# Odd tokens' rows through VectorE's block transposes, short matmuls inside products, and the first up operands queued one product earlier

## The chip, the core and the metric

The kernel runs on one core of one Trainium2 chip. A core has a matmul engine (TensorE, PE in the profile, with its weight loads as PEld), VectorE (DVE), ScalarE (ACT), GpSimd (POOL) and SyncE (SP); SP and POOL here mostly issue DMAs, and sixteen DMA engines carry these out. The metric is device time in microseconds (us) of one execution. The kernel before takes 1544.23 us, the median of three runs (1544.19 to 1544.71).

## What is computed

One decoder layer over 1024 tokens of 1024 channels, in float32. Cut to what matters here:

```python
m = jax.nn.sigmoid(sa) * y_a + jax.nn.sigmoid(sb) * y_b
x = x + jnp.einsum("bsd,de->bse", m, w_o[l])

h = rms_norm(x, g_mlp[l])
f = jnp.square(jax.nn.relu(jnp.einsum("bsd,df->bsf", h, w_1[l])))
x = x + jnp.einsum("bsf,fd->bsd", f, w_2[l])
return rms_norm(x, g_final)
```

`rms_norm` divides each token's row by the root of its mean square and multiplies by a gain per channel. Ahead of this stand a normalisation, one wide projection, a convolution branch and a recurrent branch, which give `y_a`, `y_b`, `sa` and `sb`; the change doesn't touch them. The stretch in question is the end of the `w_o` product, the second `rms_norm`, and the start of the up product with `w_1`.

## The kernel before, in words

**Layout.** In this stretch channels lie on the 128 partitions and tokens along the free axis, even tokens apart from odd ones. The residual x after the `w_o` product is held as `x1[kk, o, c2]`: kk is the half of the channels, o is 0 for even and 1 for odd tokens, c2 a pair of channel blocks; each tile is 128 x 1024 and holds two channel blocks of 512 tokens.

**Products.** A matrix product is computed as a two-by-two block product with seven products in place of eight (right blocks: channel half kk by token parity o). For each group i of output channels the products have the numbers p = 1, 2, 6, 7, 4, 5, 3. The left operands of p = 5, 6, 7, 3 are sums of weight blocks (`g_sums`, `up_lhs`), the right operands of p = 6, 7, 4, 5 differences of x blocks (`g_t`: numbers 1 to 4 of these differences).

**Precision.** Every float32 operand is split into a high part (rounded to the matmul's format) and the low rest. One product of one group is twelve matmuls over four channel blocks: high by high, high by low, low by high. For left operands ScalarE writes the negated high part, GpSimd issues a DMA that adds the source onto it (this gives the low part), and ScalarE writes the high part (`split_dma`, L63 to L67; in the profile ACT L65, POOL L66, ACT L67). For right operands ScalarE writes the high part and VectorE subtracts (`g_parts`, L1216 and L1063), except the up stage's second (gu2l, gu2h), which goes by `split_dma`.

**The sequence.** `gseq` lists 64 steps: 28 for `w_a_out` ("a"), 28 for `w_o` ("o"), and 8 for the up product ("u": p = 1 and 2 for the first four groups). The order of everything on ScalarE, VectorE, TensorE and the DMA queues is that of the program text. At step n the loop issues what follows product n - 1 (`g_post`), then product n's matmuls (`g_mm`), then the left operands of product n + 4 (`g_lhs`), the left sums of n + 5, then the extra work that the table `GX` lists for that step. Some VectorE work goes first into a list (`later`) that is sorted by an expected ready time and issued by `vector_work` or `flush`. In the names of the profile go3e is the bank of group 3 in the "o" stage, gu1a that of group 1 in the "u" stage; go_5 or gu_2 are left operands, gu1h and gu1l the right operand's two parts. After the 64 steps the up stage goes on with f0b, f1b, f0c and so on (`up_step`, L1550), product 6 first.

**The even tokens' rows and statistics.** While the "o" products run, ScalarE squares finished blocks of even x (`x1_sq`) and VectorE adds the squares (`x1_add`). At step 20 and 21 VectorE turns 32 x 32 blocks of even x (`x1_turn`, L462 STREAM_TRANSPOSE) into tiles x1r, and SP writes them with sixteen DMAs (L1394), four per tile, to `x1d` in DRAM, in runs of 128 floats; the down stage reads these rows much later. Four matmuls against a column of ones add the squares over channels (`x1_cols`, cs). `x1_root` and `x1_diag` form 1/rms by token on diagonal blocks (rdm, on VectorE and ScalarE), `x1_spread` multiplies ones with these blocks, so that each partition has every token's factor (rbm), and `x1_normed` scales x in place on VectorE (L462).

**The odd tokens' rows and statistics.** `x1_rows` does this in another way, at the first "u" step: 32 TensorE transposes into eight PSUM banks (tr), ScalarE squares each bank with a sum along the row (L1418), VectorE copies each bank into a row tile (L1422), SP writes four tiles of 128 x 1024 (L1426). Root, diagonal, spread and scaling follow as for the even ones.

**Buffers.** Most 128 x 1024 tiles come from one pool of 37 buffers:

```python
tp = ctx.enter_context(tc.tile_pool(name="acts", bufs=37))
def T(name, dt=F32, shape=(P, S)):
    return tp.tile(list(shape), dt, tag="T", name=name)
```

A new tile takes a buffer whose last tile is no longer used in the program text; the first instruction that writes it waits until the last reader of the old tile has ended, a DMA included. Which buffer a tile gets follows from the order of the requests. Eight DMA semaphores each for SP and POOL go around: a DMA is issued when the one eight before it has landed.

Of the kernel before, what the change touches and what calls it, by code (L numbers as in the profile page):

```python
# [24 lines left out]
EPS = 1e-6  # L25
# [5 lines left out]
def trunk_kernel(ctx: ExitStack, tc: tile.TileContext, x, xt_in, xt_eo, vecs, w_in, w_a_out, w_b_out,  # L31
                 w_rg, w_o, w_1, w_2, g_final, out):

    nc = tc.nc
    cp = ctx.enter_context(tc.tile_pool(name="consts", bufs=1))
# [8 lines left out]
    def T(name, dt=F32, shape=(P, S)):  # L44
        return tp.tile(list(shape), dt, tag="T", name=name)
# [8 lines left out]
    HALVES = (slice(0, HS), slice(HS, S))  # L54
# [52 lines left out]
    ident = cp.tile([P, P], F32, name="ident")  # L107
# [4 lines left out]
    ones = cp.tile([P, P], F32, name="ones")  # L112
# [671 lines left out]
    for i in range(2, NZ):  # L784
        n = zseq.index((i, 1))
# [18 lines left out]
    with tc.manual_schedule(engines=ENGINES):  # L804
        for s in range(3, NC1):
# [25 lines left out]
            c = CH[s - 1]  # L831
# [19 lines left out]
            for d in range(5):  # L851
                if s - d in EXP:
                    g = EXP[s - d]
# [36 lines left out]
    def EV(name):  # L890
        return vp.tile([P, HS], F32, tag="ev", name=name)
# [167 lines left out]
    def bank(name):  # L1059
        return zp.tile([P, HS], F32, tag="z", name=name)  # L1060
# [158 lines left out]
    def g_t(w, c2, *ns):  # L1219

        r = g_right[w]
        if 2 in ns:
            r[6, c2] = T(f"gt2{w}{c2}")
        b11, b12, b21, b22 = (r[kk, o, c2] for kk in range(2) for o in range(2))
# [41 lines left out]
    def g_mm(w, i, p):  # L1266
        b = {1: "a", 2: "a", 6: "b", 5: "e", 3: "e", 7: "f", 4: "f"}[p]
        if p in (1, 5):
            gb[w, i, b] = bank(f"g{w}{i}{b}")
        o, n = go.pop((w, i, p)), 0  # L1270
        for k in range(4):
            h, l = (a[w, p, k // 2][:, HALVES[k % 2]] for a in (gh, gl))
            for a, b_ in ((o[:, 0, k, :], h), (o[:, 0, k, :], l), (o[:, 1, k, :], h)):
                nc.tensor.matmul(gb[w, i, b], a, b_, start=p in (1, 5) and n == 0, stop=n == 11,  # L1274
                                 skip_group_check=p not in (1, 5))
                n += 1
        at("P", 12 * MM)
# [92 lines left out]
    x1d = dp.tile([8, P, D], F32, name="x1d")  # L1370


    sqs = []

    def x1_sq(i, m_):
        s = EV(f"sq{i}{m_}")
        nc.scalar.activation(s, x1[i // 2, 0, i % 2][:, HALVES[m_]], AF.Square)
        sqs.append((at("A", 0.62, clk["V"]), s))

    def x1_add(n=1):  # L1380
        for _ in range(n):
            ready, s = sqs.pop(1)
            later(ready, 0.63, tt, sqs[0][1], sqs[0][1], s, ALU.add)

    def x1_turn(kk):
        for th in range(2):
            r = T(f"x1r{kk}{th}")
            for c2 in range(2):
                src = x1[kk, 0, c2].rearrange("p (m h b j) -> p h m b j", m=2, h=2, j=32)[:, th]
                dst = r.rearrange("p (b m j) -> p m b j", m=4, j=32)[:, 2 * c2:2 * c2 + 2]  # L1390
                dve(0.65, 0, nc.vector.transpose, dst, src)
            d = x1d[2 * th:2 * th + 2].rearrange("q (b i) (k g x) -> k g i (q b) x", b=4, k=2, g=4)
            for g in range(4):
                nc.sync.dma_start(d[kk, g], r[32 * g:32 * g + 32].rearrange("p (b x) -> p b x", x=P))  # L1394

    def x1_cols():

        sqs.append(bank("cs"))
        for n in range(4):
            nc.tensor.matmul(sqs[1][:, n:n + 1], sqs[0][1][:, n * P:(n + 1) * P], ones[:, 0:1],  # L1400
                             start=True, stop=True)
        at("P", 0.9)

    def x1_rows(*ts):
        for t in ts:
            o, n = divmod(t, 4)
            if n == 0:
                rst[o] = cp.tile([P, 6, 4], F32, tag="st6", name=f"stm{o}", bufs=2)
            rows = T(f"x1r{t}")
            for kk in range(2):  # L1410
                ps = bank(f"tr{t}{kk}")
                for c in range(4):
                    nc.tensor.transpose(ps[:, c * P:(c + 1) * P],
                                        x1[kk, o, c // 2][:, c % 2 * HS + n * P:c % 2 * HS + (n + 1) * P],
                                        ident)
                at("P", 0.45)
                a = T(f"sq{t}{kk}")[:, 0:HS]
                nc.scalar.activation(a, ps, AF.Square, accum_out=rst[o][:, kk, n:n + 1])  # L1418
                at("A", 0.63, clk["P"])

                def copy(rows, kk, ps, t):
                    nc.vector.tensor_copy(  # L1422
                        rows[:, HALVES[kk]].rearrange("p (g c j) -> p c g j", g=4, c=4),
                        ps.rearrange("p (c g j) -> p c g j", g=4, c=4))
                    if kk:
                        nc.sync.dma_start(x1d[t], rows)  # L1426

                later(clk["P"], 0.63, copy, rows, kk, ps, t)
            if t == 7:
                x1_root(1)  # L1430
            if o:
                vector_work(clk["V"])

    def x1_root(o):

        if o == 0:
            rst[o] = cp.tile([P, 6, 4], F32, tag="st6", name=f"stm{o}", bufs=2)
        a, b, v, s = (rst[o][:, i, :] for i in range(4))
        if o:
            tt(v, a, b, ALU.add)  # L1440
        nc.vector.tensor_scalar(v, v if o else sqs[1][:, 0:4], 1.0 / D, EPS, ALU.mult, ALU.add)
        nc.scalar.activation(s, v, AF.Sqrt)
        at("A", 1.5)

# [163 lines left out]
    def flush():  # L1608
        vector_work(clk["V"])

    def g_get(n, f):
        return f(*gseq[n]) if 0 <= n < len(gseq) else None

# [17 lines left out]
        13: ((g_parts, "o", 4, 1),), 14: ((x1_sq, 0, 0),),  # L1631
        15: ((g_parts, "o", 5, 0), (x1_sq, 1, 0)),
        16: ((g_parts, "o", 5, 1), (x1_add,), (x1_sq, 2, 0), (up_load, 0, (0,))),
        17: ((g_parts, "o", 3, 0), (x1_add,), (x1_sq, 3, 0), (x1_sq, 0, 1), (up_load, 1, (0,))),
        18: ((g_parts, "o", 3, 1), (x1_add, 2), (x1_sq, 1, 1), (up_load, 2, (0,))),
        19: ((x1_add,), (x1_sq, 2, 1), (up_load, 3, (0,))),
        20: ((x1_add,), (x1_sq, 3, 1), (flush,), (x1_turn, 0)),
        21: ((x1_add,), (flush,), (x1_cols,), (x1_turn, 1), (up_load, 0, (1,))),
# [174 lines left out]
    ready = 4  # L1813
# [285 lines left out]
```

## Time and profile before

| what | value |
|---|---|
| median of three runs | 1544.23 us |
| the profiled execution's own time | 1544.64 us |
| its span, first to last instruction | 1542.9 us |
| granted TensorE clock | 0.999 |
| busy: TensorE, VectorE, ScalarE, GpSimd | 1533.1, 1222.5, 903.6, 184.4 us |
| first "u" product starts | 914.91 us |
| first product of the up stage proper (f0b) starts | 943.11 us |

Start times are microseconds from the span's start. A row of the view in order of time gives the start, the duration, the engine, the line, the operation, output <- input, the shape, how many were merged, and in brackets how long the engine stood idle before it and what ended that. A row of the DMA view gives the queue's engine, the count, KB of each and the median time from issue to landing; rows that begin with q0 or q1 give the two DMA queues' packets, MB and share of the sixteen engines' time in the stretch asked for. Matmuls overlap, so the time that one costs is the distance between starts: 0.23 us for 512 columns, not its duration of 0.39.

### The profile page before, as it was taken

The numbers are of one execution on the slowest core, as the hardware profiler recorded it, in microseconds if no ns is written. First come the engines' busy times: TensorE is split into PE (matmuls) and PEld (weight loads), VectorE is DVE, ScalarE is ACT, GpSimd is POOL, SyncE is SP. The second block draws the span as 40 slices with busy tenths as digits, with TensorE's granted clock in tenths as the row PEclk, the third lists the DMA queues.
The fourth block names the chain that finished last, engine by engine and source line by source line (L and its number), as shares of the span: only waits on it lengthen the run. The fifth ranks groups of instructions, "written<-read, shape, count | busy, mean of one in ns | idle before, by whom it ended". The sixth has DMA issues, their size and how long they took to land.

```text
span 1542.9 us, 19178 instructions
## 1 busy us (share of the span) xinstructions
PE 1533.1 (99%) x6782; PEld 1262.4 (82%) x6782; DVE 1222.5 (79%) x1648; ACT 903.6 (59%) x1261; POOL 184.4 (12%) x219
## 2 busy tenths in 40 slices
PE   9999999999999999999999999999999999999998
PEld 8888788888888888888888887888888888888886
DVE  6899999979899997478569879755555558888897
ACT  6648576567567667345275777554444475555553
POOL 0000000002222222000022332000000001111110
PEclk9999999999999999999999999999999999999999
DMA  8776978898997879953579898333333779888862
GB/s 347 197 189 161 251 187 222 217 280 217 247 253 196 193 191 246 327 157 116 182 201 299 197 193 204 137 122 112 113 114 111 241 216 228 223 222 224 209 130 110
DMA packets 132288, 307.82 MB, mean 200 GB/s; under 512 B 13232, under 2 KB 35248, under 8 KB 132192
## 3 DMA queue, kind: packets, MB, share of 16 engines
q1 hardware_dynamic: 101744, 230.60, 46.0%
q0 software_dynamic: 30304, 75.74, 26.9%
q8 instruction: 53, 0.87, 0.2%
q14 instruction: 43, 0.35, 0.1%
q10 hardware_dynamic: 144, 0.26, 0.0%
HBM read 147.69 MB, written 58.72 MB: 134 GB/s over the span
## 4 chain that ended last, share of the span: by engine, by line
PE 95%; DMA 2%; issue 1%; DVE 1%; SPq 0%; POOL 0%; ACT 0%; POOLq 0%; DVEq 0%
PE z L726 18%; PE d L1863 15%; PE yb L1097 8%; PE e L1983 3%; PE keep L1863 2%; PE z L258 1%; PE rg L534 1%; PE rg L536 1%; PE rg L535 1%; DMA x<-in_x_dram 1%; DMA gu<-w_raw 1%; DMA xc<-in_xt_dram 0%; PE go3f L1274 0%; PE f15d L1550 0%; PE f15c L1550 0%
## 5 line engine op out<-in xcount | busy, mean ns | idle before, releaser
L726 PE MATMUL z<-xh,win_h 128*128 128x512 f32 x400 | 124.9, 390 | 0.0
L726 PE MATMUL z<-xl,win_h 128*128 128x512 f32 x400 | 124.5, 389 | 0.0
L1875 DVE TENSOR_TENSOR acc<-acc,d 128x1024 f32<-128x1024 f32 x72 | 87.8, 1219 | 33.3 <-PE d L1863 32.6
L726 PE MATMUL z<-xh,win_l 128*128 128x512 f32 x400 | 98.2, 391 | 0.0
L726 PEld LDWEIGHTS z<-xh,win_l 128*128 128x128 f32 x400 | 75.1, 188 | 16.9
L726 PEld LDWEIGHTS z<-xh,win_h 128*128 128x128 f32 x400 | 75.0, 188 | 16.7 <-ACT win_h L67 0.7
L637 DVE SCALAR_TENSOR_TENSOR y<-u,vec,y 128x511 f32<-128x511 f32 (+14 forms) x120 | 88.3, 736 | 0.0
L726 PEld LDWEIGHTS z<-xl,win_h 128*128 128x128 f32 x400 | 75.1, 188 | 15.8
L542 ACT ACTIVATE g<-rg,vec 96x1024 f32<-96x1024 f32 x32 | 35.6, 1113 | 85.5 <-issue 46.0
L637 DVE SCALAR_TENSOR_TENSOR y<-yt,csum,y 128x511 f32<-128x511 f32 (+6 forms) x112 | 82.5, 736 | 0.0
L637 DVE SCALAR_TENSOR_TENSOR yt<-u,vec,yt 128x511 f32<-128x511 f32 (+6 forms) x112 | 82.5, 736 | 0.0
L66 POOL DMA_DIRECT2D win_l<-win_raw x25 | 21.8, 871 | 324.3 <-ACT win_l L65 312.3
L1538 ACT ACTIVATE o<-s 128x512 fp32r<-128x512 f32 x56 | 33.7, 623 | 45.7 <-DVE s L1522 26.4
L66 POOL DMA_DIRECT2D zo<-zw x42 | 36.6, 871 | 129.4 <-ACT zo L65 116.1
L1097 PE MATMUL yb<-hgl,wb_h 128*128 128x512 f32 x168 | 51.7, 389 | 0.0
L1097 PE MATMUL yb<-hgh,wb_h 128*128 128x512 f32 x168 | 51.7, 389 | 0.0
L486 DVE SCALAR_TENSOR_TENSOR v<-xb,vec,v 128x1023 f32<-128x1023 f32 (+2 forms) x36 | 46.2, 1282 | 6.9 <-ACT v L477 6.1
L66 POOL DMA_DIRECT2D db_1l<-wr x7 | 6.1, 870 | 310.5 <-ACT db_1l L65 287.9
L1097 PE MATMUL yb<-hgh,wb_l 128*128 128x512 f32 x168 | 41.0, 389 | 0.0
L65 ACT ACTIVATE zo<-zw 128x512 fp32r<-128x512 f32 x42 | 26.3, 625 | 20.7 <-PE z10f L914 2.1
L1063 DVE TENSOR_TENSOR o<-s,o 128x512 fp32r<-128x512 f32 x56 | 37.3, 683 | 0.5 <-ACT o L1538 0.5
L1097 PEld LDWEIGHTS yb<-hgh,wb_h 128*128 128x128 f32 x168 | 31.5, 188 | 6.6
(1805 smaller groups left out, 4669.7 us busy)
## 6 DMA issues: line engine op xcount, KB each, us to landing
w_raw<-in_w_dram SPq DMA_DIRECT2D x34, 512.0 KB, 5.7
fr<-fd SPq DMA_DIRECT2D x32, 512.0 KB, 6.3
wr<-in_w_dram SPq DMA_DIRECT2D x32, 512.0 KB, 6.6
zw<-in_w_in_dram SPq DMA_DIRECT2D x28, 512.0 KB, 6.3
win_raw<-in_w_in_dram SPq DMA_DIRECT2D x25, 512.0 KB, 6.8
win_l<-win_raw POOLq DMA_DIRECT2D x25, 512.0 KB, 6.7
zo<-zw POOLq DMA_DIRECT2D x42, 256.0 KB, 5.6
gates<-zg SPq DMA_DIRECT2D x32, 256.0 KB, 3.9
```

The costliest lines, as they stand in the source:

```text
L65: nc.scalar.activation(l, src, AF.Copy, scale=-1.0)
L66: nc.gpsimd.dma_start(l, src, accum_op=ALU.add)
L486: nc.vector.scalar_tensor_tensor(v[:, d:S], a[:, 0:S - d], cbw_c[:, w * 12 + t:w * 12 + t + 1], v[:, d:S], ALU.mult, ALU.add)
L542: nc.scalar.activation(a, gps.pop((n, gi))[:HD, :], AF.Sigmoid, bias=(ba_c, bx_c)[gi][:, n:n + 1])
L637: nc.vector.scalar_tensor_tensor(o[:, k:], a[:, 0:HS - k], c, o[:, k:], ALU.mult, add)
L726: nc.tensor.matmul(zps[s][:, HALVES[hf]], w[:, k, :], xw[k][part][hf], start=n == 0, stop=n == 23)
L1063: tt(l, src, h.bitcast(F32), ALU.subtract)
L1097: nc.tensor.matmul(ps[hf], a, b[:, HALVES[hf]], start=n == 0, stop=n == len(todo) - 1)
L1538: nc.scalar.activation(o[:, 0], src, AF.Copy)
L1863: nc.tensor.matmul(o, a, b, start=n == 0 and (p != 1 or g == 0), stop=n == len(todo) - 1, skip_group_check=p == 1 and g > 0)
L1875: tt(acc[p, q2], acc[p, q2], ps, ALU.add)
L1983: nc.tensor.matmul(o, a, b, start=n == 0 and t not in LOADED, stop=n == len(todo) - 1, skip_group_check=t in LOADED)
```

## The change

- Odd tokens' rows are made as the even ones: eight block transposes on VectorE in place of 32 TensorE transposes and eight copies, and sixteen row DMAs in place of four. `x1_rows` is gone; `x1_sq`, `x1_add`, `x1_turn`, `x1_cols` and `x1_root` take the parity o.
- The odd squares are made by ScalarE from x itself and added by VectorE; five of the eight go into evacuation tiles or new tiles of the pool of 37 (sqs0 and sqs6, each used in halves).
- The column sums of the odd squares and the odd spread are issued inside a product, after its sixth matmul (`G_MID`: groups 1 and 2 of the first "u" product).
- The even spread is issued one step sooner (step 22 in place of 23).
- Left operands of the "u" steps are issued five products ahead, the others four as before.
- The first sums of left blocks for the up stage (`up_lhs` with 6) come one step later, and VectorE's order of normalised blocks, transposes and differences at the "u" steps is new.

```diff
         for k in range(4):
+            if k == 2 and (w, p, i) in G_MID:
+                f, *a = G_MID[w, p, i]
+                f(*a)
...
+    sqs = {0: [], 1: []}
+    sqt = []
+
+    def x1_sq(o, i, m_):
+        n = len(sqt)
+        if o == 0 or 0 < n < 5:
+            s = EV(f"sq{o}{i}{m_}")
+        else:
+
+            if n in (0, 6):
+                x1_sq.t = T(f"sqs{n}")
+            s = x1_sq.t[:, HALVES[0 if n in (0, 6) else 1]]
+        if o:
+            sqt.append(s)
+        nc.scalar.activation(s, x1[i // 2, o, i % 2][:, HALVES[m_]], AF.Square)
+        sqs[o].append((at("A", 0.62, clk["V"]), s))
...
+    def x1_turn(o, kk, *ths):
+        for th in ths:
+            r = T(f"x1r{o}{kk}{th}")
             for c2 in range(2):
-                src = x1[kk, 0, c2].rearrange("p (m h b j) -> p h m b j", m=2, h=2, j=32)[:, th]
+                src = x1[kk, o, c2].rearrange("p (m h b j) -> p h m b j", m=2, h=2, j=32)[:, th]
                 dst = r.rearrange("p (b m j) -> p m b j", m=4, j=32)[:, 2 * c2:2 * c2 + 2]
                 dve(0.65, 0, nc.vector.transpose, dst, src)
-            d = x1d[2 * th:2 * th + 2].rearrange("q (b i) (k g x) -> k g i (q b) x", b=4, k=2, g=4)
+            t = 4 * o + 2 * th
+            d = x1d[t:t + 2].rearrange("q (b i) (k g x) -> k g i (q b) x", b=4, k=2, g=4)
             for g in range(4):
                 nc.sync.dma_start(d[kk, g], r[32 * g:32 * g + 32].rearrange("p (b x) -> p b x", x=P))
...
-    def x1_rows(*ts):
...
+    G_MID = {("u", 1, 1): (x1_cols, 1), ("u", 1, 2): (x1_spread, 1)}
...
-        22: ((x1_diag, 0), (up_load, 1, (1,))),
-        23: ((x1_spread, 0), (x1_normed, 0, 0)), 24: ((g_parts, "u", 1, 0), (g_parts, "u", 1, 1)),
-        25: ((x1_normed, 1, 0),), 26: ((g_parts, "u", 2, 0),), 27: ((g_parts, "u", 2, 1),)}.items()})
+        22: ((x1_diag, 0), (x1_spread, 0), (up_load, 1, (1,))),
+        23: ((x1_normed, 0, 0), (x1_sq, 1, 0, 1), (x1_sq, 1, 1, 1)), 24: ((g_parts, "u", 1, 0), (g_parts, "u", 1, 1), (x1_sq, 1, 2, 1)),
+        25: ((x1_normed, 1, 0), (x1_add, 1), (x1_sq, 1, 3, 1)),
+        26: ((g_parts, "u", 2, 0), (x1_add, 1, 2), (x1_sq, 1, 0, 0)),
+        27: ((g_parts, "u", 2, 1), (x1_add, 1), (x1_sq, 1, 1, 0), (x1_sq, 1, 2, 0))}.items()})
...
-        0: ((up_lhs, 0, 6), (x1_rows, 4, 5, 6, 7)),
-        1: ((x1_diag, 1),), 2: ((x1_spread, 1), (up_lhs, 1, 6)),
-        3: ((x1_normed, 0, 1), (x1_normed, 1, 1), (g_t, "u", 0, 1), (g_t, "u", 1, 1)),
-        4: ((g_t, "u", 0, 2), (g_t, "u", 1, 2)), 5: ((g_parts, "u", 6, 0),),
+        0: ((x1_sq, 1, 3, 0), (x1_add, 1, 2), (flush,), (x1_turn, 1, 0, 0), (x1_add, 1), (flush,),
+            (x1_turn, 1, 0, 1)),
+        1: ((x1_root, 1), (x1_diag, 1), (up_lhs, 0, 6)),
+        2: ((x1_normed, 0, 1), (x1_turn, 1, 1, 0, 1), (g_t, "u", 0, 1), (flush,), (x1_normed, 1, 1)),
+        3: ((g_t, "u", 0, 2), (flush,), (up_lhs, 1, 6), (g_t, "u", 1, 1)),
+        4: ((g_t, "u", 1, 2),), 5: ((g_parts, "u", 6, 0),),
...
-            g_get(n + 4, g_lhs)
+
+            for d in (4, 5):
+                if n + d < len(gseq) and (gseq[n + d][0] == "u") == (d == 5):
+                    g_get(n + d, g_lhs)
```

More of the change, by code (lines that the diff above doesn't have):

```diff
@@ L1223, in g_t @@
             r[6, c2] = T(f"gt2{w}{c2}")
-        b11, b12, b21, b22 = (r[kk, o, c2] for kk in range(2) for o in range(2))
+        b11, b12, b21, b22 = (r.get((kk, o, c2)) for kk in range(2) for o in range(2))
         for n in ns:
@@ L1370, in trunk_kernel @@
     x1d = dp.tile([8, P, D], F32, name="x1d")
[L1373 to L1380, printed above, removed]
-        for _ in range(n):
[L1382 to L1387, printed above, removed]
+    sqs = {0: [], 1: []}
@@ new lines, in trunk_kernel, with x1_add @@
+    sqt = []
[11 more added lines that the diff above has]
+        sqs[o].append((at("A", 0.62, clk["V"]), s))
+    def x1_add(o, n=1):
+        for _ in range(n):
+            ready, s = sqs[o].pop(1)
+            later(ready, 0.63, tt, sqs[o][0][1], sqs[o][0][1], s, ALU.add)
@@ L1393, in x1_turn, with x1_cols @@
             for g in range(4):
                 nc.sync.dma_start(d[kk, g], r[32 * g:32 * g + 32].rearrange("p (b x) -> p b x", x=P))
-    def x1_cols():
-        sqs.append(bank("cs"))
+    def x1_cols(o):
+        sqs[o].append(bank(f"cs{o}"))
         for n in range(4):
-            nc.tensor.matmul(sqs[1][:, n:n + 1], sqs[0][1][:, n * P:(n + 1) * P], ones[:, 0:1],
+            nc.tensor.matmul(sqs[o][1][:, n:n + 1], sqs[o][0][1][:, n * P:(n + 1) * P], ones[:, 0:1],
                              start=True, stop=True)
@@ L1402, in x1_cols @@
         at("P", 0.9)
-    def x1_rows(*ts):
[L1405 to L1432, printed above, removed]
@@ L1434, in x1_root @@
-    def x1_root(o):
[L1436 to L1441, printed above, removed]
+    def x1_root(o):
+        rst[o] = cp.tile([P, 6, 4], F32, tag="st6", name=f"stm{o}", bufs=2)
+        v, s = (rst[o][:, i, :] for i in range(2, 4))
+        nc.vector.tensor_scalar(v, sqs[o][1][:, 0:4], 1.0 / D, EPS, ALU.mult, ALU.add)
@@ L1630, in trunk_kernel @@
         10: ((g_t, "o", 0, 4), (x_in2, 1, 2, 3)), 11: ((g_t, "o", 1, 4),), 12: ((g_parts, "o", 4, 0),),
[L1631 to L1636, printed above, removed]
@@ L1637, in trunk_kernel @@
-        20: ((x1_add,), (x1_sq, 3, 1), (flush,), (x1_turn, 0)),
-        21: ((x1_add,), (flush,), (x1_cols,), (x1_turn, 1), (up_load, 0, (1,))),
-        22: ((x1_diag, 0), (up_load, 1, (1,))),
-        23: ((x1_spread, 0), (x1_normed, 0, 0)), 24: ((g_parts, "u", 1, 0), (g_parts, "u", 1, 1)),
-        25: ((x1_normed, 1, 0),), 26: ((g_parts, "u", 2, 0),), 27: ((g_parts, "u", 2, 1),)}.items()})
+        13: ((g_parts, "o", 4, 1),), 14: ((x1_sq, 0, 0, 0),),
+        15: ((g_parts, "o", 5, 0), (x1_sq, 0, 1, 0)),
@@ new lines, in trunk_kernel @@
+        16: ((g_parts, "o", 5, 1), (x1_add, 0), (x1_sq, 0, 2, 0), (up_load, 0, (0,))),
+        17: ((g_parts, "o", 3, 0), (x1_add, 0), (x1_sq, 0, 3, 0), (x1_sq, 0, 0, 1), (up_load, 1, (0,))),
+        18: ((g_parts, "o", 3, 1), (x1_add, 0, 2), (x1_sq, 0, 1, 1), (up_load, 2, (0,))),
+        19: ((x1_add, 0), (x1_sq, 0, 2, 1), (up_load, 3, (0,))),
+        20: ((x1_add, 0), (x1_sq, 0, 3, 1), (flush,), (x1_turn, 0, 0, 0, 1)),
+        21: ((x1_add, 0), (flush,), (x1_cols, 0), (x1_turn, 0, 1, 0, 1), (up_load, 0, (1,))),
```

## The prediction

> **What bounds the kernel now.** I read the page's first part, then TensorE's waits over the whole span, then TensorE in order of time around the changed steps, then the other queues there.
>
> ```profile
> span 1542.9 us, 19178 instructions
> PE 1533.1 (99%) x6782; PEld 1262.4 (82%) x6782; DVE 1222.5 (79%) x1648; ACT 903.6 (59%) x1261; POOL 184.4 (12%) x219
> ...
> PE gu1a L1274 <- DMA gu<-w_raw: 1.7, 1, 1.7
> PE spare L345 <- POOL ones L113: 1.6, 1, 1.6
> ```
>
> TensorE is busy in 99% of the span and waits twice, once of them in our stretch. So time can be won here in two ways only: less TensorE work, or that one wait; and any new wait on TensorE is paid in full. All sums below are made against this execution, whose own time is 1544.64 us (span 1542.9, 1.74 around it). The median of the three timed runs is 1544.23, so 0.41 comes off at the end.
>
> TensorE in order of time (start, duration, line, work):
>
> ```profile
> 896.71 0.95 PE L1400 MATMUL cs<-ones,sq 128*128 128x1 f32 x8
> 897.52 0.49 PE L1274 MATMUL go2e<-go5h,go 128*128 128x512 f32 x1
> 900.38 0.39 PE L1274 MATMUL go3e<-go5h,go 128*128 128x512 f32 x1
> 903.10 1.05 PE L1463 MATMUL rbm<-rdm,ones 128*128 128x128 f32 x8
> 914.91 0.39 PE L1274 MATMUL gu0a<-gu1h,gu 128*128 128x512 f32 x1
> 917.63 3.65 PE L1413 MATMUL tr<-ident,x 128*128 128x128 f32 x32
> 921.04 0.48 PE L1274 MATMUL gu1a<-gu1h,gu 128*128 128x512 f32 x1
> 926.58 1.05 PE L1463 MATMUL rbm<-rdm,ones 128*128 128x128 f32 x8
> 935.23 0.74 PE L1274 MATMUL gu1a<-gu2h,gu 128*128 128x512 f32 x2 [1.67 <-DMA gu<-w_raw]
> 943.11 0.39 PE L1550 MATMUL f0b<-gu6h,o 128*128 128x512 f32 x1
> ```
>
> The reader is to see: one product of twelve matmuls takes 2.72 (914.91 to 917.63); the transposes hold TensorE for 3.41 (917.63 to 921.04); the column sums of squares (cs) for 0.81; the wait of 1.67 comes from an up left operand whose low part arrives late. The up stage proper begins at 943.11.
>
> **The change, part by part.**
>
> *TensorE's own work.* The 32 transposes go: -3.41. Four column-sum matmuls for the odd tokens come: +0.81. The 1.67 goes if the left operands, queued one product earlier, land in time; I count it as gone. Putting short matmuls inside a product instead of between two costs nothing of its own: both places have one switch in and one out.
>
> *Even spread one step sooner.* It moves from 903.10 to where go3e starts, 900.38. Its operand is made here:
>
> ```profile
> 900.35 0.70 ACT L1455 ACTIVATE rdm<-ident,stm 128x128 f32<-128x128 f32 x2 [0.29 <-DVE stm L105]
> ```
>
> ScalarE's second diagonal block ends at 901.05, so the last of the four spread matmuls starts then and not at 900.38 + 0.6. TensorE waits between 0 and 0.5; I take +0.3. VectorE gets its normalised rows 2.4 us sooner, which TensorE doesn't see by itself.
>
> *VectorE.* Out go eight copies, in come eight block transposes and seven additions of squares:
>
> ```profile
> 892.67 2.49 DVE L462 STREAM_TRANSPOSE x1r<-x 128x512 f32<-128x512 f32 x4
> 895.08 0.65 DVE L462 TENSOR_TENSOR x<-xe,go0e 128x512 f32<-128x512 f32 x1
> ...
> 907.43 2.35 DVE L1063 TENSOR_TENSOR gu1l<-x,gu1h 128x1024 fp32r<-128x1024 f32 x2
> 909.70 0.68 DVE L462 TENSOR_TENSOR x<-xe,go0e 128x512 f32<-128x512 f32 x1
> ...
> 919.42 3.68 DVE L1422 COPY x1r<-tr 128x512 f32<-128x512 f32 x6 [2.29 <-ACT sq L1418]
> ```
>
> A transpose costs 0.60 (four in 2.41), a copy 0.61 (3.68 / 6), a 512-wide addition 0.60, a 1024-wide one 1.13. So the exchange is even and the additions are +4.2 us on VectorE. [...]
>
> *The wait that is added.* This decides. The built programs name for every wait the semaphore and its count, and so the instruction waited for. Tiles of the large pool go to whoever asks next, and the first writer waits for the last user. In before, the four tiles of even rows (x1r) went to gu2_1, gu2l1, gu2h1 and gu0_2, the fourth to gu0_2, which ScalarE reaches only at 916.64 (the last row of the second fence below). In the changed kernel a tile for squares and earlier left operands come first, and the fourth tile goes to gu2_1, the left operand of the third up product. ScalarE writes it first, so ScalarE waits until that tile's row write has landed:
>
> ```profile
> 907.11 1.89 SPq L1394 DMA_DIRECT2D x1d<-x1r  x1
> ...
> x1d<-x1r SPq DMA_DIRECT2D x1, 128.0 KB, 6.1
> ```
>
> 907.11 + 6.1 = 913.2. ScalarE comes to gu2_1 much sooner. Its rows:
>
> ```profile
> 889.94 0.63 ACT L1377 ACTIVATE sq<-x 128x512 f32<-128x512 f32 x1 [1.52 <-DVE x L462]
> 890.48 0.62 ACT L65 ACTIVATE go<-wo 128x512 fp32r<-128x512 f32 x1
> ...
> 900.95 0.62 ACT L65 ACTIVATE go<-wo 128x512 fp32r<-128x512 f32 x1
> ...
> 908.48 0.62 ACT L67 ACTIVATE gu<-w_raw 128x512 fp32r<-128x512 f32 x1
> 909.00 0.62 ACT L65 ACTIVATE gu<-w_raw 128x512 fp32r<-128x512 f32 x1
> ...
> 914.74 1.05 ACT L65 ACTIVATE gu2l<-x 128x1024 fp32r<-128x1024 f32 x1
> 915.69 1.04 ACT L67 ACTIVATE gu2h<-x 128x1024 fp32r<-128x1024 f32 x1
> 916.64 0.61 ACT L65 ACTIVATE gu<-w_raw 128x512 fp32r<-128x512 f32 x1
> ```
>
> A square costs 0.54 from start to start, half a left operand 0.52, a 1024-wide copy 0.95. From 900.95 ScalarE has six half operands (go3, gu0, gu1: 3.1), three squares (1.6) and two gu1h copies (1.9): it stands at gu2_1 at 907.6 and waits 5.6 us or more. Queued behind it are eight half operands (4.16), four 1024-wide copies (3.8) and five squares of odd tokens (2.7): 10.66 us. VectorE then has the last additions and two transposes left, about 1.2 more, and only then can the odd column sums start on TensorE: 11.9 us after the tile is free.
>
> How late is it free? Nothing ahead of that write moves except the low part of gu1_1. ScalarE ends its source at about 904.6 (900.95 + 2 x 1.04 + 2 x 0.54 + 0.52), so GpSimd issues it near 904.7 instead of 909.02.
>
> ```profile
> 909.02 1.77 POOL L66 DMA_DIRECT2D gu<-w_raw  x2 [5.25 <-ACT gu L65]
> ...
> DMA packets 993, 0.48 MB, mean 240 GB/s; under 512 B 57, under 2 KB 993, under 8 KB 993
> ...
> q0 software_dynamic: 128, 0.24, 68.2%
> q1 hardware_dynamic: 232, 0.11, 34.5%
> ...
> q0 software_dynamic: 183, 0.41, 109.3%
> ...
> DMA packets 229, 0.78 MB, mean 392 GB/s; under 512 B 26, under 2 KB 26, under 8 KB 229
> ```
>
> (Stretches of 2 us: the row writes alone at 899, both queues at 905, the accumulating queue alone at 919, the whole-row writes of before at 927.) While both queues have work, the accumulating one (q0) has twice the share of the row writes. A low part of 256 KB at 0.41 MB per 2 us is 1.3 us of all engines. So the tile is free between 913.2 and 914.5; one queue serves gu1_1 after gu0_1, so only part of it falls ahead: I take 914.0. [...]
>
> So cs can start at 914.0 + 11.9 = 925.9. TensorE would be ready for it at 914.91 + 0.3 + 2.72 + 1.36 = 919.3. The wait: +6.6.
>
> *After it.* TensorE and VectorE now both run from the odd spread. In before VectorE ended the first sixth operand at 939.3, 4.0 us ahead of its use (second matmul of f0b, 943.11 + 0.23):
>
> ```profile
> 927.67 5.35 DVE L462 SCALAR_TENSOR_TENSOR x<-x,vec,rbm 128x512 f32<-128x512 f32 x8
> ...
> 938.09 1.22 DVE L1063 TENSOR_TENSOR gu6l<-gt2u,gu6h 128x1024 fp32r<-128x1024 f32 x1
> ```
>
> Of these 4.0, 1.67 go with TensorE's old wait, and 1.36 come back because the spread stands half a product earlier. But four transposes (2.4) and three sums of left blocks (1.9) now lie inside: 4.0 - 1.7 + 1.4 - 4.3 = -0.6. Also ScalarE's queue now has o1_6 ahead of gu6h, waiting for a sum that VectorE ends late, and u1_3 behind that, on which gu3a's second product waits. Followed through, f0b's second matmul comes 1.5 late, its eighth 0.8 more (ScalarE makes the second gu6h after another product's output), and f0d another 1.0 (VectorE's seventh operand). Each lies between 0 and twice that. Sum +3.3, on the path.
>
> *Hidden.* The odd row writes on SP stand ahead of the product outputs and of the next weight loads; before's outputs had only four writes ahead. Nothing needs the rows before the down stage. I cost them at nothing, 2 us if the weights then come late.
>
> **Sum:** -3.41 - 1.67 + 0.81 + 0.3 + 6.6 + 3.3 = +5.9, so 1550.5 on this execution's scale and 1550.1 on that of the median.
>
> **The rivals.**
>
> *The wait isn't met* (2 in 10), the one on the faster side. If the fourth tile's write lands before about 908, ScalarE never stops, its last square ends near 918.3 and cs starts nearly on time. Then the sum is -3.41 - 1.67 + 0.81 + 0.3 = -4.0 if VectorE keeps up as well (1540.3), and about -0.7 + 0.2 with its lateness (1543.7). For it: the moved steps are placed for exactly this. Against it: the landing at 913.2 is measured, and no step ahead of that write gets shorter. The point from which it decides: each us of landing after 908 is a us on TensorE, so 914.0 - 5.9 = 908.1 is where the gain is used up.
>
> *DMA late as well* (2 in 10). [...] Price 2 to 4 more: 1552 to 1554. [...]
>
> *It doesn't do what it says:* "five ahead" queues gu2_1 sooner in ScalarE's order, and has it written later (913 instead of 909). That is part of my forecast and no case of its own.
>
> **How the numbers follow.** Forecast 6 in 10: landing 913.2 to 916 and the later waits between half and one and a half of 3.3 give 1547.5 to 1553. The range takes in most of the late-DMA case and the slower half of the first rival: 1543.5 to 1554. A measurement of this kernel can tell about 0.2%, 3.1 us, from no change, so faster means under 1541.1 and slower over 1547.3. Faster: 0.08, the better end of the first rival. Within: 0.19, the rest of that rival and a small part of the forecast. Slower: 0.73.
>
> **What would show it.** In the profile of the changed kernel: no tr rows and four more cs matmuls; an idle time of ScalarE of 5 to 7 us ending near 914 ahead of a gu operand, released by x1d; a TensorE wait of about 6.6 at cs, released by VectorE's addition of squares; no wait of gu1a for its low part; short waits at gu3a and f0b. I am wrong if ScalarE doesn't stand still between 907 and 913, or if cs starts before 921.

## The result, and the profile after

The changed kernel takes 1554.96 us, the median of four runs (1554.54 to 1555.53), against 1544.21 for the kernel before beside it (1543.59 to 1544.71): a ratio of 1.0069, 95% interval 1.0053 to 1.0085. It is 10.75 us slower, where +5.9 was forecast; the range ended at 1554.0.

TensorE's waits over the whole span of the changed kernel (engine, what waited, line, what it waited for, us in total, times, longest):

```profile
span 1552.8 us, 19140 instructions
...
PE cs L1414 <- DVE sqs L462: 5.5, 1, 5.5
PE spare L345 <- POOL ones L113: 1.6, 1, 1.6
PE f0d L1531 <- DMA o<-s: 1.6, 1, 1.6
PE gu3a L1277 <- ACT u L1331: 0.8, 1, 0.8
PE f0b L1531 <- DVE gu6l L1063: 0.4, 1, 0.4
```

The old wait of gu1a for a low part is gone. In its place stand a wait of 5.5 us at the odd column sums and three smaller ones behind it. ScalarE in order of time shows where the long one comes from:

```profile
907.44 0.61 ACT L1390 ACTIVATE sq<-x 128x512 f32<-128x512 f32 x1
913.45 0.63 ACT L65 ACTIVATE gu<-w_raw 128x512 fp32r<-128x512 f32 x1 [5.39 <-DMA x1d<-x1r]
...
923.50 0.61 ACT L1390 ACTIVATE sqs<-x 128x512 f32<-128x512 f32 x1
```

ScalarE stands still for 5.39 us ahead of a left operand (gu2_1), until the write of a row tile (x1d<-x1r) has landed. The last odd square starts 10.05 us after the operand. Then TensorE, in order of time:

```profile
919.55 0.39 PE L1277 MATMUL gu1a<-gu1h,gu 128*128 128x512 f32 x1
925.48 1.84 PE L1414 MATMUL cs<-ones,sqs 128*128 128x1 f32 x8 [5.55 <-DVE sqs L462]
927.18 0.77 PE L1277 MATMUL gu1a<-gu1h,gu 128*128 128x512 f32 x1
927.76 0.63 PE L1277 MATMUL gu1a<-gu1l,gu 128*128 128x512 f32 x1
...
932.42 1.05 PE L1444 MATMUL rbm<-rdm,ones 128*128 128x128 f32 x8
933.23 0.48 PE L1277 MATMUL gu2a<-gu1h,gu 128*128 128x512 f32 x1
```

Read the starts. The column sums take 1.70 (925.48 to 927.18) where the even ones take 0.81. The twelve matmuls from there to the spread take 5.24 (927.18 to 932.42) where twelve took 2.82 in before (921.04 to 923.86). Matmuls that wait for nothing have become slower. The view of busy time by windows has the granted clock in its third column of numbers (length, busy and instructions ahead of it; the DMA share and GB/s behind it):

```profile
919.90:925.40 5.50, 0.04 (x1) 0.70 1.05 191
925.40:932.40 7.00, 6.92 (x20) 0.50 1.01 187
932.40:936.00 3.60, 3.60 (x21) 1.00 1.05 200
```

During the wait the clock of TensorE falls (0.70 over the wait), and the first 7 us of work after it run at half speed (0.50).

The code ahead of the even column sums is the same in all kernels here, yet in the profiled executions these sums start anywhere from 896.71 to 898.53 us. So I compare one stretch: from the first even column sum to the first matmul of f2b. Before's three parts of it (to gu0a, to f0b, to f2b), then those of the changed kernel:

```profile
896.71:914.91 18.20, 18.20 (x90) 1.00 1.00 206
914.91:943.11 28.20, 26.53 (x137) 1.00 0.88 220
943.11:970.31 27.20, 27.20 (x121) 1.00 0.89 217
```

```profile
897.13:915.70 18.57, 18.48 (x90) 1.00 1.00 222
915.70:949.42 33.72, 27.36 (x113) 0.85 0.84 164
949.42:979.97 30.55, 28.44 (x122) 1.00 0.80 196
```

The stretch grew from 73.60 to 82.84 us, by 9.24; the span grew by 9.9, with 0.42 of the rest ahead of the stretch.

### The profile page after: what moved, and what is told of

Same layout as the page of the kernel before. It is cut to its first block, busy times and chain, and to the rows that moved or that the text cites. A ratio compares the mean times of both kernels' runs of the same rounds, so it can differ in the third digit from the quotient of the medians.

```text
span 1552.8 us, 19140 instructions
## 1 busy us (share of the span) xinstructions
PE 1535.5 (99%) x6758; PEld 1261.7 (81%) x6758; DVE 1227.4 (79%) x1654; ACT 903.0 (58%) x1253; POOL 184.8 (12%) x219
## 4 chain that ended last, share of the span: by engine, by line
PE 94%; issue 2%; DMA 2%; DVE 1%; ACT 1%; POOL 0%; SPq 0%; POOLq 0%; DVEq 0%; ACTq 0%
PE z L726 18%; PE d L1853 15%; PE yb L1097 8%; PE e L1973 3%; PE keep L1853 2%; PE z L258 1%; PE rg L534 1%; PE rg L536 1%; PE rg L535 1%; DMA x<-in_x_dram 1%; DMA o<-s 0%; DMA xc<-in_xt_dram 0%; DMA x1d<-x1r 0%; PE go3f L1277 0%; PE f15d L1531 0%
## 5 line engine op out<-in xcount | busy, mean ns | idle before, releaser
L1097 PEld LDWEIGHTS yb<-hgl,wb_h 128*128 128x128 f32 x168 | 31.5, 188 | 6.6
```

The source lines that it names most:

```text
L1097: nc.tensor.matmul(ps[hf], a, b[:, HALVES[hf]], start=n == 0, stop=n == len(todo) - 1)
```

## The experiments

Theory A: the write of the fourth row tile holds ScalarE at gu2_1, the odd squares queue behind it, and TensorE's wait at the column sums costs its length and a stretch at half clock. Rival B: the longer list of VectorE and the added row writes make the up stage late, whatever ScalarE does. Each kernel below was timed beside the kernel before. "Stretch" is the one above, in the kernel's profiled execution; 73.60 is before, 82.84 the change. Each stretch and each row of waits is one execution, and those of e1, e3, e4, e5 and e7 took 1.2 to 2.8 us longer than the kernel's median, so the medians decide and small differences between stretches don't.

| kernel | median, us | beside it, before | ratio (95%) | stretch, us |
|---|---|---|---|---|
| e1_spread_later | 1549.85 | 1543.88 | 1.0046 (1.0034 to 1.0059) | 78.39 |
| e2_keep_warm | 1552.01 | 1543.88 | 1.0053 (1.0040 to 1.0066) | 79.80 |
| e3_four_ahead | 1553.86 | 1543.88 | 1.0061 (1.0046 to 1.0077) | 81.81 |
| e4_before_five_ahead | 1546.51 | 1543.88 | 1.0022 (1.0013 to 1.0031) | 77.96 |
| e5_sum_sooner | 1547.02 | 1543.75 | 1.0015 (1.0006 to 1.0024) | 76.36 |
| e6_no_odd_rows | 1546.42 | 1543.75 | 1.0015 (1.0006 to 1.0024) | 74.23 |
| e7_squares_first | 1545.80 | 1543.75 | 1.0011 (1.0002 to 1.0020) | 74.19 |
| e8_late_rows | 1543.66 | 1543.76 | 1.0000 (0.9992 to 1.0009) | 70.57 |
| e9_fourth_tile_unwritten | 1546.43 | 1543.76 | 1.0017 (1.0007 to 1.0026) | 75.32 |
| e10_rows_later_still | 1544.85 | 1544.12 | 1.0008 (0.9999 to 1.0017) | 70.62 |
| e11_rows_last | 1544.75 | 1544.12 | 1.0003 (0.9994 to 1.0012) | 70.80 |
| e12_spread_behind | 1543.31 | 1544.23 | 0.9992 (0.9983 to 1.0001) | 71.57 |

### Whose buffer: e1 and e9

e1 undoes one line of the change:

```diff
-        22: ((x1_diag, 0), (x1_spread, 0), (up_load, 1, (1,))),
-        23: ((x1_normed, 0, 0), ...
+        22: ((x1_diag, 0), (up_load, 1, (1,))),
+        23: ((x1_spread, 0), (x1_normed, 0, 0), ...
```

> The changed kernel with one thing undone: the spread of the even tokens' factors stands behind go3e again, where it stood before. In this build the row tiles are handed to other operands: gu2_1 gets a tile of go5l1, and the fourth row tile goes to gu2l1, which ScalarE reaches some 4 us later. Theory A (the write of the row tile holds ScalarE, TensorE then waits for the odd squares and its clock falls): ScalarE's wait of 5.4 goes, TensorE waits 1 to 2.5 at the odd column sums instead of 5.5 and stays at full clock, the later waits at gu3a, f0b and f0d (4 us in all) mostly stay; 1544 to 1547.5 us. Theory B (the odd rows' writes and VectorE's longer list make the up stage late whatever ScalarE does): over 1551 us.

e9 leaves the spread where the change put it and takes the writes of the fourth tile away:

```diff
+            if (o, kk, th) == (0, 1, 1):
+                continue
             t = 4 * o + 2 * th
...
```

The down stage of e9 reads other rows in place of those.

> The changed kernel with the row writes of the fourth even tile left out (the last stage reads other rows in their place, so the output lacks them); the even spread stays where the change put it. gu2_1 then gets the third row tile, whose last write is issued four writes (3.7 us) sooner. Theory A (ScalarE waits for the landing of the tile that it gets): its wait is still there, released by a row write, but ends 3 to 4.5 us sooner; the odd column sums start 3 to 4.5 us sooner, and 3 to 6 us go: 1549 to 1552. Theory B (the landing is a coincidence, ScalarE is held by something else at 913.4): same time, 1554 to 1556.

ScalarE around gu2_1 in e1, then in e9:

```profile
908.48 0.61 ACT L1390 ACTIVATE sq<-x 128x512 f32<-128x512 f32 x1
909.00 0.62 ACT L65 ACTIVATE gu<-w_raw 128x512 fp32r<-128x512 f32 x1
```

```profile
907.97 0.61 ACT L1390 ACTIVATE sq<-x 128x512 f32<-128x512 f32 x1
909.55 0.63 ACT L65 ACTIVATE gu<-w_raw 128x512 fp32r<-128x512 f32 x1 [0.96 <-DMA x1d<-x1r]
```

With another buffer the wait is gone; with the third row tile it is there, but 0.96 long, and ends 4.4 us sooner (11.89 us after the even column sums, 16.32 in the change). So it is the landing of the tile that the operand inherits. In both, the odd column sums come sooner as well (3.9 and 4.4 us, against the even ones), and the medians are 5.1 and 8.5 us under the change's. That is theory A; B has no place for it. It isn't the whole loss: the medians are still 6.0 and 2.7 us over before's beside them. (e9 also takes four writes off the DMA queues; e1 doesn't.)

Both sizes were missed. e9 gained more than I allowed, since its remaining wait of 1.15 left the clock at 1.00 (from 921.6 to 927.6). e1 gained less. Its wait is the 2.0 that was expected, but I expected full clock after it, and the row of the windows from 923 on says 0.50:

```profile
919.70:921.70 2.00, 0.02 (x1) 1.00 1.09 214
921.70:923.00 1.30, 1.30 (x10) 1.00 1.12 217
923.00:926.00 3.00, 3.00 (x9) 0.50 1.05 203
```

### The clock by itself: e2

```diff
...
         sqs[o].append(bank(f"cs{o}"))
+        if o:
+            l, r = hot   # operands of the product around it
+            for n in range(22):
+                nc.tensor.matmul(sqs[o][1], l, r, start=True, stop=True)
...
```

> The changed kernel with 22 more matmuls of 128x512 on TensorE just ahead of the odd column sums, whose result is overwritten: they fill 5 us of its wait and nothing waits for them. Theory A (the idle time of 5.5 us makes the granted clock fall to 0.5, and TensorE pays about 0.9 more at the column sums and 2.4 in the matmuls up to the spread): the clock stays at 1.0, the rest of the wait is under 1 us, and the kernel is 2.3 to 3.3 us faster than the changed one: 1551.5 to 1552.8. Theory B (the half clock comes from something else, or what it costs is waited for later anyway): within 1 us of 1555, or more.

TensorE in e2:

```profile
919.49 5.15 PE L1417 MATMUL cs<-gu1h,gu 128*128 128x512 f32 x22
925.44 1.05 PE L1419 MATMUL cs<-ones,sqs 128*128 128x1 f32 x8 [0.80 <-DVE sqs L462]
926.36 0.48 PE L1278 MATMUL gu1a<-gu1h,gu 128*128 128x512 f32 x1
```

The column sums start where they did (28.57 after the even ones; 28.35 in the change) and take 0.92 instead of 1.70, and the matmuls behind them are 0.23 apart. The stretch is 3.04 shorter with 22 matmuls more in it. The waits behind them hardly moved: gu3a, f0b and f0d wait 0.8, 0.4 and 1.8 (0.8, 0.4 and 1.6 in the change). Theory A: keeping TensorE busy with work that is thrown away wins what the half clock cost.

### The other part of the order: e3 and e4

e3 is the change, and e4 the kernel before, each with the other's distance for the "u" operands:

```diff
-            for d in (4, 5):
-                if n + d < len(gseq) and (gseq[n + d][0] == "u") == (d == 5):
-                    g_get(n + d, g_lhs)
+            g_get(n + 4, g_lhs)
```

> The changed kernel with the up left operands queued four products ahead again. gu2_1 still gets the fourth row tile and gu1_1 now gets the third. Theory A (the wait for the tile sets the end, and what is queued behind it on ScalarE the rest): two half operands less stand between gu2_1 and the last odd square, so the odd column sums start 1 to 1.6 us sooner; 1552 to 1554. Theory B (five ahead is what hurts): the wait of ScalarE goes, under 1549. If the old wait for a low part comes back beside all this, 1556 to 1557.

> The kernel before with the up left operands queued five products ahead and nothing else. gu2_1 gets the first row tile, which has landed by then. If one product's more time is enough for the low parts, TensorE's wait of 1.67 goes: 1542.3 to 1543. If the low parts stand in a queue that is full either way, the wait stays: 1544 to 1545.

e3 can't be told from the change (the intervals overlap). ScalarE's wait for the tile stays, 5.25 us; five ahead isn't what hurts. The shorter list behind it didn't show, since the tile also landed later (17.5 us after the even column sums, 16.3 in the change).

e4 went a way that neither theory had: the wait for the low part is gone, and the kernel is slower, by a ratio of 1.0022. TensorE now stops inside the transposes:

```profile
917.87 3.22 PE L1413 MATMUL tr<-ident,x 128*128 128x128 f32 x28
925.17 1.12 PE L1413 MATMUL tr<-ident,x 128*128 128x128 f32 x4 [4.09 <-DVE x1r L1422]
925.94 0.78 PE L1274 MATMUL gu1a<-gu1h,gu 128*128 128x512 f32 x1
```

The reason is a load of up weights, two DMAs issued from 909.1 in before and from 909.9 in e4. Here are their rows in the view of DMAs from 908 to 916, before and then e4, and then VectorE's wait in e4:

```profile
w_raw<-in_w_dram SPq DMA_DIRECT2D x2, 512.0 KB, 7.7
```

```profile
w_raw<-in_w_dram SPq DMA_DIRECT2D x2, 512.0 KB, 12.4
```

```profile
DVE s L1521 <- DMA w_raw<-in_w_dram: 5.2, 1, 5.2
```

With the low parts queued sooner the load takes 4.7 us longer, and its second DMA is issued 1.5 us later (911.2 against 909.7). VectorE's left sum waits for it, ScalarE's o0_6 waits for the sum, the squares of the transposed rows stand behind o0_6, and the last transposes wait for a free bank. The clock falls here too: it is 0.98 over the stretch, where before has 1.00, and behind the wait matmuls of 512 columns start 0.43 apart (926.51 to 926.94) and not 0.23. "One product earlier" moves a transfer; it doesn't only remove a wait. The size is not that of every execution: the profiled one took 1549.34, 2.8 over the median, and nine of the eleven timed ones show a mean clock of 0.999 or 1.000 where it shows 0.998, so the fall of the clock can't be seen in most of them.

### What makes the later waits: e5, e6 and e7

All three start from e1. e5 moves one entry of the table, from two steps later:

```diff
-        1: ((x1_root, 1), (x1_diag, 1), (up_lhs, 0, 6)),
+        1: ((x1_root, 1), (x1_diag, 1), (up_lhs, 0, 6), (up_lhs, 1, 6)),
...
```

> As e1_spread_later, and the sums for the left operand o1_6 are asked for right behind those for o0_6, ahead of the odd normed rows, transposes and left blocks on VectorE. In e1 ScalarE stood 9.3 us for them with u1_3 and both gu6h queued behind. Theory A (the later waits at gu3a, f0b, f0c and f0d come from this order): gu3a's 0.8 goes, gu6h and gu6l come sooner, and at least half of the later 4 us goes; 1546 to 1548. Theory B (VectorE's longer list itself makes the sixth operand late): only gu3a's wait goes and f0b waits for it instead; 1549 to 1550.

e6 returns at once from `x1_turn` for odd tokens, so their rows are neither turned nor written, and the down stage reads the even ones in their place:

> As e1_spread_later with the odd tokens' transposes and row writes left out (the last stage then reads the even tokens' rows in their place, so the output lacks the odd rows). VectorE has 4.8 us less to do here (8 x 0.60) and SP 16 writes less. Theory B (VectorE's added work is what makes the later waits): f0b, f0c and f0d no longer wait, the odd column sums start 0.6 sooner; 1545 to 1546.5. Theory A (the order behind o1_6 does it): gu3a and f0b still wait; 1548 to 1549.5.

e7 is e5 with ScalarE's order changed at the end, and one pair of transposes behind the odd diagonal:

```diff
-        27: ((g_parts, "u", 2, 1), (x1_add, 1), (x1_sq, 1, 1, 0), (x1_sq, 1, 2, 0))
+        27: ((x1_add, 1), (x1_sq, 1, 1, 0), (x1_sq, 1, 2, 0))
...
-        0: ((x1_sq, 1, 3, 0), (x1_add, 1, 2), (flush,), (x1_turn, 1, 0, 0), (x1_add, 1), (flush,),
-            (x1_turn, 1, 0, 1)),
+        0: ((x1_sq, 1, 3, 0), (x1_add, 1, 3), (flush,), (x1_turn, 1, 0, 0), (g_parts, "u", 2, 1),
+            (g_lhs, "u", 1, 2)),
+        1: ((x1_root, 1), (x1_diag, 1), (x1_turn, 1, 0, 1), ...
...
```

> As e5_sum_sooner, and on ScalarE the last odd squares stand ahead of the second half of the gu2 operand and of gu1_2; one pair of transposes moves behind the odd diagonal. Theory A (what is queued on ScalarE between the even rows and the last odd square sets when the column sums start, and a wait of 2 us with short matmuls behind it lowers the clock): the last square ends near 918.5, the column sums wait under 0.7 us, the clock stays 1.0, and 2.5 to 4 us go against e5: 1542.5 to 1545. Theory B (VectorE sets the end from the odd spread on, so what TensorE gains ahead of it is waited for at f0b): within 1.5 us of e5.

TensorE's waits in e1, e5, e6 and e7 (those of this stretch):

```profile
PE cs L1414 <- DVE sqs L462: 2.0, 1, 2.0
...
PE f0c L1531 <- DMA o<-s: 1.3, 1, 1.3
...
PE f0d L1531 <- DVE gu7l L1063: 0.8, 1, 0.8
PE gu3a L1277 <- ACT u L1331: 0.8, 1, 0.8
PE f0b L1531 <- DVE gu6l L1063: 0.4, 1, 0.4
PE f1d L1531 <- DMA o<-s: 0.3, 1, 0.3
```

```profile
PE cs L1414 <- DVE sqs L462: 2.7, 1, 2.7
...
PE f0d L1531 <- DVE gu7l L1063: 0.8, 1, 0.8
```

```profile
PE cs L1416 <- DVE sqs L462: 1.5, 1, 1.5
...
PE f0d L1533 <- DMA o<-s: 0.6, 1, 0.6
PE f0c L1533 <- DMA o<-s: 0.2, 1, 0.2
```

```profile
PE f0b L1531 <- DVE gu6l L1063: 1.5, 1, 1.5
PE cs L1414 <- DVE sqs L462: 0.6, 1, 0.6
PE f0d L1531 <- DMA o<-s: 0.6, 1, 0.6
PE rbm L1444 <- DVE rdm L1434: 0.4, 1, 0.4
```

e5 and e6 each take the waits at gu3a and f0b away, by different means: the order behind o1_6, and VectorE's work. So these waits need both, and neither theory is enough alone. e6 left transposes and writes out at once; the writes alone were not tried. In e7 the wait at cs is 0.6 and the clock stays at 1.00, as A has it, and the stretch is 2.2 shorter than e5's. But f0b waits 1.5 for VectorE, and the median is only 1.2 under e5's (the intervals overlap), as B has it: part of what TensorE gains ahead of the odd spread it gives back behind it.

### Paying for VectorE's work elsewhere: e8, e10, e11 and e12

e8 is e7 with two edits of VectorE's list:

```diff
+        1: ((x1_root, 1), (x1_turn, 1, 0, 1), (x1_diag, 1), (up_lhs, 0, 6), (up_lhs, 1, 6)),
+        2: ((x1_normed, 0, 1), (g_t, "u", 0, 1), (flush,), (x1_normed, 1, 1)),
...
-            hq[kk, o, c2] = src = a = x1[kk, o, c2]
+            src = x1[kk, o, c2]
+            hq[kk, o, c2] = a = T(f"xn{c2}") if kk and o else src
...
+          9: ((x1_turn, 1, 1, 0),), 11: ((x1_turn, 1, 1, 1),)}   # of the up stage's products
```

> As e7_squares_first, with VectorE's list ahead of the sixth operand cut by 3.6 us: one pair of odd transposes stands in the 1.7 us in which VectorE waited for the root, and the last four (2.4 us) come after the up stage's first products, which is possible because the normed rows of that half go to tiles of their own instead of over the old ones. Theory B of e6 and e7 (from the odd spread on VectorE sets the end): f0b no longer waits for gu6l (2.2 us in e7), the stretch from the even column sums to f2b falls from 74.2 to 71.5 to 72.5 (73.6 before), 1542 to 1543.5 us. Theory A (something other than VectorE is as late: the o operands' low parts): f0b or f0c waits for those instead, stretch over 73.5, 1545 or more.

e10 and e11 move these transposes behind products 15 and 18, or 20 and 24, issue the odd column sums after nine matmuls of gu1a, and put the odd spread between gu2a and gu3a. In both, the odd normed rows are multiplied with the diagonal blocks in place of the spread factors, because the scaling was issued ahead of the spread; they do the same amount of work and lack one wait. e12 is e11 with the spread ahead of the scaling.

> As e8_late_rows; the last four odd transposes come after the 15th and the 18th product of the up stage proper instead of the 9th and 11th (in e8 f2c waited 1.0 for an addition of VectorE just behind them), the odd column sums go in three matmuls later and the odd spread at the end of gu2a, where TensorE no longer waits for either (0.6 and 0.5 in e8). Theory A (what is left over in e8 are these three waits): 2 us less than e8; 1541 to 1542.5. Theory B (each wait taken away comes back at the next product that needs VectorE): 1543 to 1544.5.

> As e10_rows_later_still, with those transposes after the 20th and 24th product, where VectorE has 40 to 55% idle time. If e10 still has a wait behind its transposes, this one is 0.5 to 1.2 us faster than e10; if not, both are the same within 0.4; if the tiles that are held longer make a load of weights late, it is slower than e10.

> As e11_rows_last, but the odd normed rows wait for the odd spread again: in e10 and e11 they were multiplied with the diagonal blocks instead of the spread factors (their output is therefore not the reference's) and so did not wait for TensorE's spread. Here the spread stands between gu2a and gu3a and the normed rows behind it. VectorE starts them about 0.5 us later than in e11 and ends gu6l some 1.5 us ahead of its use. Theory A (the stretch has slack now): like e11 within 1 us, no wait at the odd column sums and the spread, 1543 to 1544.5, that is, not to be told from the kernel before. Theory B: f0b waits for gu6l again, over 1545.

TensorE's waits in e8, then in e12:

```profile
PE f2c L1532 <- DVE fa L1558: 1.0, 1, 1.0
PE cs L1414 <- DVE sqs L462: 0.6, 1, 0.6
PE rbm L1444 <- DVE rdm L1434: 0.5, 1, 0.5
```

```profile
PE gu3a L1277 <- DMA gu<-w_raw: 2.1, 1, 2.1
```

In e8 every wait at f0b, f0c and f0d is gone and the stretch is 3.0 us under before's, more than forecast. That is the gain in this stretch alone, with the last four transposes moved out of it. The median is level with before all the same. In the profiled executions 0.56 of the 3.0 is lost ahead of the stretch, where the code is the same, 1.2 at f2c behind the moved transposes, and 0.5 in small pieces later; the span (1542.2) is 0.7 under before's, whose profiled execution stood 0.4 above its median. e10 and e11 settled less than hoped: their waits at cs and the spread are gone, but e10 now waits 1.1 at gu3a for a low part, and e11 0.3 there and 0.7 at f0d. Their medians still can't be told from before's (1.0008 and 1.0003, with 1 in both intervals). That is nearer to theory B of e10, though 1544.85 lies above its range. In e12 a wait for a low part is back at gu3a, of the kind that cost 1.67 in before. The best version, e12, stands at 0.9992 (0.9983 to 1.0001): not to be told from the kernel before.

## Why the prediction was wrong

The direction and the mechanism were right, and so was the place of every term but one. Against the rows:

| step of the prediction | forecast, us | measured, us |
|---|---|---|
| transposes, column sums, old DMA wait | -3.41 +0.81 -1.67 | gone, there, gone |
| even spread one step sooner | +0.3 | +0.37 (18.57 - 18.20) |
| row tile free, ScalarE moves on | 914.0 | 913.45 |
| odd column sums start | 925.9 | 925.48 |
| wait at them | +6.6 | +5.55 |
| half clock behind the wait | not there | +3.31 (0.89 + 2.42) |
| gu3a, f0b, f0c, f0d | +3.3 | +4.16 (0.81 + 1.14 + 0.32 + 1.89) |

**The step that failed** stands in the first part: "any new wait on TensorE is paid in full". It is paid in full and then some. The 3.31 are what 1.70 at the column sums and 5.24 in the next twelve matmuls are over 0.81 and 2.82. e2 took them away alone: its stretch is 3.04 and its median 2.95 shorter. With them the forecast would have been +9.2, and the span grew by 9.9. In before no window of this stretch has a clock under 1.00: its wait of 1.67 left it there (1.00 from 933 to 939). That was no bound for the 6.6 that I forecast, four times as long, and I set none.

What was missing is in the traces: TensorE was at half its clock (0.50) for 10.24 us, which began inside the wait of 5.55. A shorter wait had it too: in e6 one of 1.52 was followed by 3.4 us at half clock. The last section has both.

**The wait itself** was 1.05 shorter than forecast: the sums started 0.42 sooner, and TensorE was ready at 919.93 and not at 919.3 (0.42 of that because its whole stretch started later than before's). That short matmuls inside a product cost no more than between two was nearly so: the odd column sums took 0.89 in e12, where they didn't wait (920.25 to 921.14), and the even ones 0.81.

**The later waits** were 0.9 more than forecast. gu3a and f0b waited for what was named. f0d waited for the low part of an o operand, and not for VectorE's seventh operand; e1 has both waits. No run takes that low part's lateness away by itself, so what made it late stays open.

**The sum.** The table counts idle time for the old wait, the wait at cs and gu3a. From start to start they cost 2.00, 5.70 and 1.11, and with these the terms add up to the 9.24 of the stretch. The forecast took the first of them at 1.67.

**The rival "the wait isn't met"** was priced wrongly too. e1 comes near that case (its even spread stands in the old place): ScalarE doesn't stop for the tile, yet it takes 1549.85 and not 1540.3 to 1543.7. Two operands ahead of the odd squares still wait 0.27 and 0.54 for VectorE's rows, cs waits 2.0, the clock falls after it, and the later waits stay. e9 keeps the spread and stops for only 0.96; it takes 1546.43. Only when the squares, the sums and the transposes were moved as well (e8) did the stretch fall by 3.0, where this rival's better end promised 4.0.

**The rival "DMA late as well"** was partly true: a wait of 1.6 at f0d was for a DMA, and e4 shows a weight load late by 4.7 us when low parts come sooner. No run shows the 2 to 4 us that it was priced at. From 925 to 942 the change has the odd rows' sixteen writes in place of one whole-row write; the DMA engines moved 178 GB/s, 228 in before, but the low parts of the "u" operands landed 5.3 us after their issue, 9.2 in before, and that of the o operand 4.5, 9.1 in before (medians of one to three each).

## What to carry to other kernels

A new tile from a pool waits for whoever used its buffer last. So after a change of order look up, in the built program, which buffer each tile of a blocked engine inherits, above all whether its last reader is a DMA. Price a wait on TensorE at its length, and look at the clock behind it: here a wait of 5.55 us cost another 3.31 in work at half clock, and one of 1.52 (e6) had 3.4 us at half clock behind it, by estimate 1.7 us lost if all of them are filled with work. Dense work that is thrown away may be cheaper than standing still: in e2 it took 3.04 us off the stretch. Work taken off a saturated engine is won only as far as the engine that takes it over is ahead of its next deadline: here VectorE had none to spare between the odd statistics and f0b, and even behind f2b the moved transposes cost 1.0 at f2c (e8) until they were moved further (e11).

## What the hardware showed

The clock fell sooner and stayed down longer than I would have thought. In the change it dropped 2.2 us into the idle time (1.00 from 921.5 to 922.0, 0.64 from 922.0 to 922.5). It was back some 6.9 us after the first column sum, 5.2 us after the dense matmuls began again (0.62 from 932.0 to 932.5). In e6 it fell behind a wait of only 1.52: it was 1.00 until 922.5, well after work had begun again (920.96), and 0.50 from 923 to 926. Behind the waits of 1.15 in e9 (1.00 from 921.6 to 927.6) and 1.67 in before (1.00 from 933 to 939) it didn't fall.

**How long it lasted.** The clock was 1.00 or 0.50 in the windows around a fall and a return, so the mean of the window in which it changes gives the moment:

| kernel | windows of the fall and the return | falls, us | back, us | at half clock, us |
|---|---|---|---|---|
| the change | 922.0 to 922.5: 0.64; 932.0 to 932.5: 0.62 | 922.14 | 932.38 | 10.24 |
| e1 | 923.0 to 926.0: 0.50; 926.0 to 926.5: 0.59 | 923.00 | 926.41 | 3.41 |
| e6 | 922.5 to 923.0: 0.76; 926.0 to 926.5: 0.82 | 922.76 | 926.18 | 3.42 |

In e3, e5 and e4 the mean clock of the stretch is 0.96, 0.96 and 0.98. By estimate from these and the lengths of the stretches (81.81, 76.36 and 77.96), some 6.5, 6.1 and 3.1 us of each were at half clock.

**What goes with a fall.** The length of the wait alone doesn't part the kernels: 1.52 in e6 had the half clock behind it, and 1.67 in before and 2.05 in e12 (1.00 over its whole stretch) hadn't. What differs is the work beside the wait: matmuls of 512 columns on both sides of it in before and e12, and eight column sums of one column behind it in e6, e1 and the change. But these stand behind the wait of 1.15 in e9 as well. No run changes the work beside a wait alone, so what decides isn't shown.

A load of weights of 512 KB took 7.7 us to land in before and 12.4 in e4, where the left operands were queued one product sooner and nothing else was changed; the DMA engines were at 0.88 to 1.09 of their time in before while it ran (stretches of 2 us from 909 to 917).
